# A decoder layer on one core: decay differences per head on VectorE and ScalarE, and no `wlo` of the convolution's weights on GpSimd

## The chip, the core and the metric

The kernel runs on one core of a Trainium2 chip. Five engines work side by side, each with a queue of its own that runs strictly in order: TensorE (PE; its weight loads are listed as PEld), VectorE (DVE), ScalarE (ACT), GpSimd (POOL) and SyncE (SP), which issues most of the transfers. The metric is the device time of one execution in microseconds, as a median of runs.

## The reference

One hybrid decoder layer in float32 on 256 tokens of width 1024: a half-step feed-forward part, then two token mixers side by side, cross-attention to a memory, and a second feed-forward part, each with a residual and a layer norm. The change touches one mixer, the state-space branch. Its inputs go through a causal convolution of width 4 and a silu, and its decay is a difference of running sums for each of 16 heads:

```python
def segsum(a):
    l = a.shape[-1]
    cs = jnp.cumsum(a, axis=-1)
    diff = cs[..., :, None] - cs[..., None, :]
    mask = jnp.tril(jnp.ones((l, l), dtype=bool))
    return jnp.where(mask, diff, -jnp.inf)
...
    xbc = jax.nn.silu(causal_dwconv(xbc, conv_w, conv_b))
...
    dt = jax.nn.softplus(dt_raw.astype(jnp.float32) + dt_bias)
...
    decay_in = jnp.exp(segsum(a))
    y_diag = jnp.einsum('bcgls,bgrcls,bcsgrp->bclgrp', cb, decay_in, xdt)
    decay_to_end = jnp.exp(a_cs[..., -1:] - a_cs)
```

Chunks are 128 tokens long, so there are two of them (`tb` 0 and 1 in the kernel).

## The kernel before

Every weight piece, 128x1024 in float32, is loaded into `raw` (4 buffers) by SP, rounded by ACT into `whi` and completed by `wlo = raw - whi` (6 buffers each), as `split` does at lines 150 and 151; PE multiplies in three passes (`mm3`: whi by high, whi by low, wlo by high). The subtraction runs on DVE, but `weight(ap, pool=True)` gives the second piece of a pair to POOL.

In the stage of the change, `fly` runs four streams against each other, and a scheduler then fixes the order of each engine's queue: `ssd_decay` (softplus of the time steps, their running sums `cs` by a matmul with a triangle, and the two tiles `E`), `latent` (`wb`, transposed and stored as `cTh` and `cTl`), `xbc` (the convolution), and `k_index`. `xbc` takes eight units of two pieces each, `u` = 4, 5, 6, 7 and then 0, 1, 2, 3, with POOL for the second piece of every odd `u`. The pieces are called m0 to m15 below, in the order of use, so POOL makes m3, m7, m11 and m15. Behind each unit's matmuls come, for each of two blocks of 128 channels, a bias step on ACT (line 454), three convolution steps on DVE (line 456) and a silu on ACT (line 458). Blocks 8 to 15, which come first, stay in `bcT`; blocks 0 to 7 (`wa`, 4 buffers; "token blocks" below) are transposed on PE by `flush` and copied into `xtok`.

In `ssd_decay`, POOL writes the transposed sums to DRAM (line 560), reads them back to all 128 partitions as `E` (16 heads x 128, line 562), and subtracts `cs` there (line 563). In `ssd`, DVE clips E at 0 from above (line 599), ACT takes its exponential (lines 575 and 604), and PE multiplies with it. `issue_after(x)` puts instructions of x's engine behind x in that engine's queue. The next stages take `w_qidx` and `w_ukv` pieces the same way.

Of the kernel before, what the change touches and what calls it, by code (L numbers as in the profile page):

```python
# [21 lines left out]
AF = mybir.ActivationFunctionType  # L22
ALU = mybir.AluOpType
AX = mybir.AxisListType

P = 128
# [6 lines left out]
H = 16  # L33
# [17 lines left out]
class Layer:  # L51
# [381 lines left out]
    def xbc(self, xT, xtok, bc):  # L433

        nc, t = self.nc, self.t
        late = []

        def flush(n):
            for b, v in (late.pop(0) for _ in range(min(n, len(late)))):
                tp = self.psum("t")[:, :T].rearrange("p (b c) -> p b c", c=P)  # L440
                for tb in range(NTB):
                    self.transpose(tp[:, tb, :], v[:, tb * P:(tb + 1) * P])
                nc.scalar.copy(xtok[:, :, b * P:(b + 1) * P], tp)
        for u in (4, 5, 6, 7, 0, 1, 2, 3):
            ps = self.psum("mm")
            for _ in self.a_steps(ps, t["w_xbc"][u], xT, u % 2 == 1):
                flush(max(0, len(late) - 2))
                yield 0.0
            for i in range(2):
                b = 2 * u + i  # L450
                src = ps[:, i * T:(i + 1) * T]
                v = self.small([P, T], "wa", bufs=4) if b < 8 else bc[:, b - 8, :]
                cw = self.conv_w[:, b, :]
                nc.scalar.activation(v, src, AF.Identity, bias=self.conv_b[:, b:b + 1], scale=cw[:, 3:4])
                for d in (1, 2, 3):
                    self.last_conv = nc.vector.scalar_tensor_tensor(  # L456
                        v[:, d:], src[:, :T - d], cw[:, 3 - d:4 - d], v[:, d:], op0=ALU.mult, op1=ALU.add)
                self.last_silu = nc.scalar.activation(v, v, AF.Silu)
                if b < 8:
                    late.append((b, v))  # L460
            yield 0.0
        yield "kidx"
        flush(len(late))
# [70 lines left out]
    def ssd_decay(self):  # L534

        nc = self.nc
        hb = lambda i: self.hv[:, None, i * H:(i + 1) * H].to_broadcast([P, NTB, H])
        dt = self.dtr
        nc.vector.tensor_tensor(dt, dt, hb(0), op=ALU.add)
        self.softplus(dt.rearrange("p a b -> p (a b)"), NTB * H)  # L540
        ea = self.small([P, H], "ea", bufs=1)
        nc.scalar.activation(ea, self.hv[:, H:2 * H], AF.Exp)
        dA = self.small([P, NTB, H], "dA", bufs=1)
        nc.vector.scalar_tensor_tensor(dA, dt, -1.0, ea[:, None, :].to_broadcast([P, NTB, H]),
                                       op0=ALU.mult, op1=ALU.mult)
        yield 14.0
        csp = self.psum("t")[:, :NTB * H]
        self.mm(csp, self.triu, dA.rearrange("p a b -> p (a b)"))
        cs = self.cs = self.small([P, NTB, H], "cs", bufs=1)
        nc.vector.tensor_copy(cs, csp.rearrange("p (a b) -> p a b", b=H))  # L550
        yield 1.5
        csT_p = self.psum("t")
        csT = self.small([P, T], "wa", bufs=4)[:H].rearrange("p (a b) -> p a b", b=P)
        for tb in range(NTB):
            self.transpose(csT_p[:H, tb * P:(tb + 1) * P], cs[:, tb, :])
        nc.vector.tensor_copy(csT, csT_p[:H, :T].rearrange("p (a b) -> p a b", b=P))
        scr = self.dp.tile([NTB, H * P], F32, name="cs_rows")
        self.E = []
        for tb in range(NTB):
            nc.gpsimd.dma_start(scr[tb].rearrange("(h l) -> h l", l=P), csT[:, tb, :])  # L560
            e = self.big((7, 9)[tb], F32, (P, H, P), "E")
            nc.gpsimd.dma_start(e.rearrange("p h l -> p (h l)"), scr[tb].partition_broadcast(P))
            nc.gpsimd.tensor_tensor(e, e, cs[:, tb, :].unsqueeze(2).to_broadcast([P, H, P]), op=ALU.subtract)
            self.E.append(e)

    def ssd(self, zs, xtok, bc, yT):

        nc = self.nc
        cs, E, dt, dskip = self.cs, self.E, self.dtr, self.hv[:, 2 * H:3 * H]
# [2 lines left out]
        S0, xe = sx[:, 0, :], sx[:, 1, :]  # L572
        dte, ecs = (self.small([P, H], tag, bufs=1) for tag in ("dte", "ecs"))
        with self.tc.issue_after(self.last_silu.ins):
            nc.scalar.activation(dte, E[0][:, :, P - 1], AF.Exp)
            nc.scalar.activation(ecs, cs[:, 1, :], AF.Exp)
        bcast = lambda v, n: v.unsqueeze(2).to_broadcast([P, n, HD])
        hview = lambda v: v.rearrange("p (h d) -> p h d", d=HD)
# [11 lines left out]
        for tb in range(NTB):  # L590
            ts = slice(tb * P, (tb + 1) * P)
            e = E[tb]
            cb = self.psum("t").rearrange("p (g c) -> p g c", c=P)
            for g in range(G):
                self.mm(cb[:, g, :], bc[:, g, ts], bc[:, 4 + g, ts])
            cbm = self.small([P, G, P], "w2b", bufs=2)
            nc.vector.tensor_tensor(cbm, cb, self.triu[:, None, :].to_broadcast([P, G, P]), op=ALU.mult)
            with self.tc.issue_after(self.last_conv.ins):
                nc.vector.tensor_scalar(e, e, 0.0, None, op0=ALU.min)
            yield 0.0  # L600
            for half in range(2):
                hs = slice(half * 8, half * 8 + 8)
                with self.tc.issue_after(self.last_silu.ins):
                    nc.scalar.activation(e[:, hs, :], e[:, hs, :], AF.Exp)
                ev = e[:, hs, :].rearrange("p (g r) l -> p g r l", g=2)
                nc.vector.tensor_tensor(ev, ev, cbm[:, 2 * half:2 * half + 2, :].unsqueeze(2).to_broadcast(
                    [P, 2, H // G, P]), op=ALU.mult)
            yield SSD_US[tb]
        for half in range(2):
            ps = self.psum("mm")  # L610
# [4 lines left out]
        for tb in range(NTB):  # L615
            ts = slice(tb * P, (tb + 1) * P)
            e, yt = E[tb], xtok[:, tb, :]
            for half in range(2):
                s = slice(half * 512, (half + 1) * 512)
                ps = self.psum("mm")  # L620
# [4 lines left out]
                if tb == 1:  # L625
                    po = self.psum("mm")
                    for g in (2 * half, 2 * half + 1):
# [3 lines left out]
                                            op=ALU.mult)  # L631
# [9 lines left out]
            for g in range(G):  # L641
                nc.scalar.activation(yt[:, g * 256:(g + 1) * 256], yt[:, g * 256:(g + 1) * 256], AF.Copy,
                                     scale=rs[:, g:g + 1])
# [434 lines left out]
```

## Time and profile before

| what | value |
|---|---|
| median of 3 runs | 815.27 us (815.12 to 815.87) |
| the profiled execution | 814.78 us, of which the span of the profile is 812.9 us |
| PE busy | 789.4 us, 97% of the span |
| DVE, ACT, POOL busy | 592.4, 448.4 and 68.2 us |

The profile is of one execution. Times in it count from the start of the span. A row of a timeline gives the start, the duration, the engine, the line of the kernel, the operation, `out<-in`, the shapes and, where several equal ones follow each other, their count; in brackets stands how long the engine was idle before it and what ended that. A PE row is pipelined, so rows overlap. [...] The stage of the change runs from about 227 to 290 us.

### The profile page before, as it was taken

What the parts mean: (1) busy time and instruction counts of PE and PEld (TensorE: products, weight loads), DVE (VectorE), ACT (ScalarE), POOL (GpSimd) and SP (SyncE); (2) the same over time, 40 slices, a digit from 0 to 9 for tenths busy, and PEclk for the clock granted to TensorE, in tenths of its full rate; (3) what the DMA queues carried; (4) which work ended last, traced back from release to release, by engine and by line L of the source; (5) the groups of instructions that cost most, each with busy time, mean ns of one, the idle gap of its engine ahead of it and who ended that gap; (6) DMA issues with size and microseconds to landing.
All of it is one profiled execution on the core that took longest, in us unless ns stands there. A gap on an engine that the chain in (4) does not pass through costs nothing.

```text
span 812.9 us, 13145 instructions
## 1 busy us (share of the span) xinstructions
PE 789.4 (97%) x5070; PEld 717.5 (88%) x5070; DVE 592.4 (73%) x960; ACT 448.4 (55%) x782; POOL 68.2 (8%) x69
## 2 busy tenths in 40 slices
PE   8999999999989998989999999999999999999996
PEld 5888888887889997989999998899988988888885
DVE  4868776448588989698889767965659777776445
ACT  5756565433476684477667644544444666565330
POOL 1100000000032451230000000200002000000000
PEclk9999999999999999799999999999999999999999
DMA  7876555553656621236444456574433755555531
GB/s 249 271 267 224 193 182 194 187 200 104 210 189 228 208 74 51 81 108 233 165 150 135 158 175 215 170 276 161 156 120 134 256 191 195 192 184 194 192 105 53
DMA packets 39919, 142.90 MB, mean 176 GB/s; under 512 B 4592, under 2 KB 4896, under 8 KB 39472
## 3 DMA queue, kind: packets, MB, share of 16 engines
q1 hardware_dynamic: 38016, 134.63, 49.4%
q0 software_dynamic: 1840, 7.43, 2.9%
q8 instruction: 40, 0.66, 0.3%
q14 instruction: 23, 0.19, 0.1%
HBM read 140.97 MB, written 1.06 MB: 175 GB/s over the span
## 4 chain that ended last, share of the span: by engine, by line
PE 74%; DVE 11%; issue 8%; ACT 4%; DMA 2%; POOL 1%; SPq 0%; DVEq 0%; ACTq 0%; POOLq 0%
PE ps_mm L116 69%; DVE wlo L151 3%; PE ps_t L116 2%; PE ps_t L120 2%; DMA raw<-in_ffn_in_dram 2%; ACT whi L150 1%; PE ps_s L116 1%; DVE acc L695 1%; DVE acc L702 1%; DVE wa L456 1%; DVE m L701 1%; DMA raw<-in_w_pssd_dram 0%; POOL rstd L289 0%; DVE kv L794 0%; DVE kv L793 0%
## 5 line engine op out<-in xcount | busy, mean ns | idle before, releaser
L151 DVE TENSOR_TENSOR wlo<-raw,whi 128x1024 fp32r<-128x1024 f32 (+2 forms) x245 | 301.0, 1231 | 129.1 <-ACT whi L150 125.1
L150 ACT CAST whi<-raw 128x1024 fp32r<-128x1024 f32 (+2 forms) x253 | 263.2, 1044 | 188.1 <-PE ps_mm L116 124.6
L116 PE MATMUL ps_mm<-x1T,whi 128*128 128x256 f32 x768 | 143.9, 288 | 0.0
L116 PE MATMUL ps_mm<-x0T,whi 128*128 128x512 f32 x352 | 123.7, 400 | 2.9 <-ACT whi L150 2.1
L116 PEld LDWEIGHTS ps_mm<-x1T,whi 128*128 128x128 f32 x768 | 122.3, 195 | 0.0
L116 PE MATMUL ps_mm<-x1T,wlo 128*128 128x256 f32 x384 | 110.2, 287 | 0.0
L116 PE MATMUL ps_mm<-x3T,whi 128*128 128x512 f32 x304 | 105.6, 392 | 0.0
L116 PE MATMUL ps_mm<-x0T,wlo 128*128 128x256 f32 x352 | 97.0, 282 | 0.3 <-DVE wlo L151 0.3
L116 PE MATMUL ps_mm<-x3T,wlo 128*128 128x256 f32 x304 | 85.1, 280 | 0.0
L116 PEld LDWEIGHTS ps_mm<-x0T,whi 128*128 128x128 f32 x352 | 65.8, 188 | 20.6 <-ACT whi L150 3.6
L116 PEld LDWEIGHTS ps_mm<-x1T,wlo 128*128 128x128 f32 x384 | 75.1, 195 | 0.0
L116 PEld LDWEIGHTS ps_mm<-x3T,whi 128*128 128x128 f32 x304 | 56.9, 187 | 12.4
L116 PEld LDWEIGHTS ps_mm<-x0T,wlo 128*128 128x128 f32 x352 | 65.7, 189 | 1.6 <-DVE wlo L151 1.4
L116 PE MATMUL ps_mm<-whi,ah 128*128 128x512 f32 x154 | 60.2, 391 | 0.0
L116 PE MATMUL ps_mm<-wlo,ah 128*128 128x512 f32 x154 | 60.1, 390 | 0.0
L116 PE MATMUL ps_mm<-whi,al 128*128 128x512 f32 x154 | 59.9, 389 | 0.0
L116 PEld LDWEIGHTS ps_mm<-x3T,wlo 128*128 128x128 f32 x304 | 57.5, 189 | 0.0
L289 POOL TENSOR_TENSOR rstd<-rstd,mhalf 128x1 f32<-128x1 f32 (+1 forms) x12 | 11.3, 941 | 537.0 <-DVE rstd L288 537.0
L177 DVE TENSOR_TENSOR wa<-wa,ps_mm 128x256 f32<-128x256 f32 x82 | 34.0, 418 | 30.2 <-ACT wa L176 30.1
L347 ACT ACTIVATE wa<-wa 128x256 f32<-128x256 f32 x41 | 17.1, 417 | 48.1 <-DVE wa L177 48.1
L116 PEld LDWEIGHTS ps_mm<-whi,al 128*128 128x128 f32 x154 | 28.9, 188 | 6.2
L116 PEld LDWEIGHTS ps_mm<-whi,ah 128*128 128x128 f32 x154 | 29.0, 188 | 5.6
(296 smaller groups left out, 1551.5 us busy)
## 6 DMA issues: line engine op xcount, KB each, us to landing
raw<-in_ffn_in_dram SPq DMA_DIRECT2D x87, 512.0 KB, 4.1
raw<-in_ffn_out_dram SPq DMA_DIRECT2D x44, 512.0 KB, 3.5
raw<-in_w_xbc_dram SPq DMA_DIRECT2D x16, 512.0 KB, 4.3
raw<-in_w_gate_dram SPq DMA_DIRECT2D x16, 512.0 KB, 3.4
raw<-in_w_z_dram SPq DMA_DIRECT2D x8, 512.0 KB, 3.6
raw<-in_w_qidx_dram SPq DMA_DIRECT2D x8, 512.0 KB, 3.9
raw<-in_w_q_dram SPq DMA_DIRECT2D x8, 512.0 KB, 3.5
raw<-in_w_pssd_dram SPq DMA_DIRECT2D x8, 512.0 KB, 4.6
```

Source lines behind the costliest of these rows:

```text
L116: self.nc.tensor.matmul(out, a, b, start=start, stop=stop)
L120: self.nc.tensor.transpose(out, in_, self.ident)
L150: self.nc.scalar.copy(hi, src)
L151: (engine or self.nc.vector).tensor_sub(lo, src, hi.bitcast(F32))
L177: self.nc.vector.tensor_add(out, out, ps[:, :T])
L289: self.nc.gpsimd.tensor_tensor(v, v, self.mhalf[:, :n], op=ALU.pow)
L347: nc.scalar.activation(sg, self.join(gate, sg), AF.Silu)
L456: self.last_conv = nc.vector.scalar_tensor_tensor(v[:, d:], src[:, :T - d], cw[:, 3 - d:4 - d], v[:, d:], op0=ALU.mult, op1=ALU.add)
L695: nc.vector.scalar_tensor_tensor(acc[:, s], rl[:, s], self.widx[:, tb, h:h + 1], prev[:, s], op0=ALU.mult, op1=ALU.add)
L701: nc.vector.max(m8, acc[:, s])
L702: nc.vector.match_replace(out=acc[:, s], in_to_replace=m8, in_values=acc[:, s], imm_value=KILL)
```

## The change

The subtraction of `cs` from E leaves POOL. A new method does it in the stage of the convolution: heads 0 to 7 on DVE, subtraction and clip in one instruction per head; heads 8 to 15 on ACT, as a Relu of `cs - E`, so that these hold the negative of the clipped difference, and the exponentials take a scale of -1 for them. The DVE instructions are put behind the last convolution step of units 2 and 3; the ACT instructions have no such bond. The two clips on whole tiles go. And `xbc` no longer asks for POOL, so DVE makes m3, m7, m11 and m15 too. POOL's later `wlo` pieces, of the gate weights, stay.

```diff
@@ xbc
-            for _ in self.a_steps(ps, t["w_xbc"][u], xT, u % 2 == 1):
+            for _ in self.a_steps(ps, t["w_xbc"][u], xT):
...
+            if u in (2, 3):
+                with self.tc.issue_after(self.last_conv.ins):
+                    self.decay_steps(u - 2)
             yield 0.0
@@ ssd_decay
             nc.gpsimd.dma_start(e.rearrange("p h l -> p (h l)"), scr[tb].partition_broadcast(P))
-            nc.gpsimd.tensor_tensor(e, e, cs[:, tb, :].unsqueeze(2).to_broadcast([P, H, P]), op=ALU.subtract)
             self.E.append(e)
+
+    def decay_steps(self, tb):
+
+        e, cs = self.E[tb], self.cs
+        for h in range(H // 2):
+            self.nc.vector.tensor_scalar(e[:, h, :], e[:, h, :], cs[:, tb, h:h + 1], 0.0, op0=ALU.subtract, op1=ALU.min)
+        for h in range(H // 2, H):
+            self.nc.scalar.activation(e[:, h, :], e[:, h, :], AF.Relu, scale=-1.0, bias=cs[:, tb, h:h + 1])
@@ ssd
-            nc.scalar.activation(dte, E[0][:, :, P - 1], AF.Exp)
+            for half in range(2):
+                hs = slice(half * 8, half * 8 + 8)
+                nc.scalar.activation(dte[:, hs], E[0][:, hs, P - 1], AF.Exp, scale=(1.0, -1.0)[half])
...
-            with self.tc.issue_after(self.last_conv.ins):
-                nc.vector.tensor_scalar(e, e, 0.0, None, op0=ALU.min)
...
-                    nc.scalar.activation(e[:, hs, :], e[:, hs, :], AF.Exp)
+                    nc.scalar.activation(e[:, hs, :], e[:, hs, :], AF.Exp, scale=(1.0, -1.0)[half])
```

DVE's queue where the convolution begins, before. `wlo_2374` is m6; `sps`, `spq` and `spp` are steps of the softplus behind its exponential, and `bcT` rows are convolution steps.

```order
L523 TENSOR_SCALAR sps_2100<-spe_2099 128x32
L524 RECIPROCAL sps_2100<-sps_2100 128x32
L525 TENSOR_TENSOR sps_2100<-sps_2100,spe_2099 128x32
L526 TENSOR_TENSOR spq_2101<-sps_2100 128x32
L527 TENSOR_SCALAR spp_2102<-spq_2101 128x32
L151 TENSOR_TENSOR wlo_2374<-raw_2372,whi_2373 128x1024
L529 SCALAR_TENSOR_TENSOR spp_2102<-spp_2102,spq_2101 128x32 x3
L456 SCALAR_TENSOR_TENSOR bcT_2097<-ps_mm_2140,feat,bcT_2097 128x255
L529 SCALAR_TENSOR_TENSOR spp_2102<-spp_2102,spq_2101 128x32
L456 SCALAR_TENSOR_TENSOR bcT_2097<-ps_mm_2140,feat,bcT_2097 128x254
```

The same place after the change, from the piece m6 on; `wlo_2380` is m7, formerly POOL's.

```order
L151 TENSOR_TENSOR wlo_2374<-raw_2372,whi_2373 128x1024
L526 TENSOR_SCALAR sps_2100<-spe_2099 128x32
L527 RECIPROCAL sps_2100<-sps_2100 128x32
L528 TENSOR_TENSOR sps_2100<-sps_2100,spe_2099 128x32
L529 TENSOR_TENSOR spq_2101<-sps_2100 128x32
L530 TENSOR_SCALAR spp_2102<-spq_2101 128x32
L151 TENSOR_TENSOR wlo_2380<-raw_2378,whi_2379 128x1024
L532 SCALAR_TENSOR_TENSOR spp_2102<-spp_2102,spq_2101 128x32
L456 SCALAR_TENSOR_TENSOR bcT_2097<-ps_mm_2140,feat,bcT_2097 128x255
```

The five softplus steps now stand behind m6, not ahead of it, m7 stands between them and the chain's multiplications, and the first convolution step follows one `spp`, not three.

ACT's queue at its first table load of this stage, before (`whi_2373` is m6; `spe` is the softplus's exponential):

```order
L490 ACTIVATE wa_2132,css_2133<-wb_2085 128x256
L522 ACT_TABLE_LOAD
L522 ACTIVATE spe_2099<-spe_2099 128x32
L150 CAST whi_2373<-raw_2372 128x1024
L150 CAST whi_2379<-raw_2378 128x1024
```

and after:

```order
L493 ACTIVATE wa_2132,css_2133<-wb_2085 128x256
L150 CAST whi_2373<-raw_2372 128x1024
L525 ACT_TABLE_LOAD
L525 ACTIVATE spe_2099<-spe_2099 128x32
L150 CAST whi_2379<-raw_2378 128x1024
```

The conversion of m6 moved ahead of the table load.

ACT's queue where the token blocks begin, after the change. `E_2415` and `E_2418` are the two E tiles, `wa_2515` and `wa_2521` the first two token blocks, `whi_2705` is m15:

```order
L454 ACTIVATE bcT_2097<-ps_mm_2371,feat 128x256
L574 ACTIVATE E_2415<-E_2415,cs_2352 128x128
L454 ACTIVATE wa_2515<-ps_mm_2454,feat 128x256
L574 ACTIVATE E_2415<-E_2415,cs_2352 128x128 x6
L458 ACTIVATE bcT_2097<-bcT_2097 128x256
L574 ACTIVATE E_2415<-E_2415,cs_2352 128x128
L150 CAST whi_2705<-raw_2704 128x1024
L458 ACTIVATE wa_2515<-wa_2515 128x256
L454 ACTIVATE wa_2521<-ps_mm_2454,feat 128x256
L574 ACTIVATE E_2418<-E_2418,cs_2352 128x128 x4
L454 ACTIVATE wa_2588<-ps_mm_2527,feat 128x256
L574 ACTIVATE E_2418<-E_2418,cs_2352 128x128 x2
```

None of the `L574` rows stood there before; the bias steps, silus and m15 between them did. Two more `L574` rows and the silu of the second token block follow.

## Rows read from the trace of the kernel before

**Rows 1.** The page, its first part: busy time, share of the span, instructions.

```profile
PE 789.4 (97%) x5070; PEld 717.5 (88%) x5070; DVE 592.4 (73%) x960; ACT 448.4 (55%) x782; POOL 68.2 (8%) x69
```

**Rows 2.** PE's timeline where it transposes in the stage of the change.

```profile
243.91 0.48 PE L120 MATMUL ps_t<-ident,wb 128*128 128x128 f32 x1 [3.10 <-DVE cTl L501]
...
270.02 0.60 PE L120 MATMUL ps_t<-ident,wa 128*128 128x128 f32 x4
...
277.39 0.44 PE L120 MATMUL ps_t<-ident,wa 128*128 128x128 f32 x2 [0.80 <-ACT wa L458]
```

**Rows 3.** Windows: length, busy us (count) by PE, PEld, DVE, ACT, POOL; clock share; DMA.

```profile
243.86:247.27 3.41, 3.35 (x16) 3.36 (x17) 3.13 (x6) 2.26 (x6) 0.00 (x0) 0.50 0.24 96
247.27:250.69 3.42, 3.42 (x31) 3.42 (x31) 2.19 (x6) 1.60 (x4) 0.22 (x1) 1.00 0.77 211
...
325.78:336.02 10.24, 10.24 (x46) 9.88 (x46) 6.67 (x12) 2.99 (x5) 0.00 (x0) 0.50 0.41 148
```

**Rows 4.** DVE's timeline.

```profile
227.41 2.14 DVE L539 TENSOR_TENSOR dtr<-dtr,hv 128x32 f32<-128x32 f32 x1
229.48 1.21 DVE L151 TENSOR_TENSOR wlo<-raw,whi 128x1024 fp32r<-128x1024 f32 x1
...
235.84 2.72 DVE L529 SCALAR_TENSOR_TENSOR spp<-spp,spq 128x32 f32<-128x32 f32 x3
...
243.52 0.34 DVE L501 SCALAR_TENSOR_TENSOR cTl<-ps_t,feat,cTh 128x128 fp32r<-128x128 f32 x1
...
265.42 2.08 DVE L151 TENSOR_TENSOR wlo<-raw,whi 128x1024 fp32r<-128x1024 f32 x1 [0.90 <-ACT whi L150]
...
268.84 2.01 DVE L151 TENSOR_TENSOR wlo<-raw,whi 128x1024 fp32r<-128x1024 f32 x1
...
272.19 3.21 DVE L151 TENSOR_TENSOR wlo<-raw,whi 128x1024 fp32r<-128x1024 f32 x1
...
291.57 1.23 DVE L599 TENSOR_SCALAR E<-E 128x2048 f32<-128x2048 f32 x1
...
296.75 3.73 DVE L695 SCALAR_TENSOR_TENSOR acc<-wa,widx,caus 128x256 f32<-128x256 f32 x2
```

**Rows 5.** POOL's timeline.

```profile
226.68 2.83 POOL L151 TENSOR_TENSOR wlo<-raw,whi 128x1024 fp32r<-128x1024 f32 x1 [0.96 <-ACT whi L150]
...
235.88 2.41 POOL L151 TENSOR_TENSOR wlo<-raw,whi 128x1024 fp32r<-128x1024 f32 x1 [2.99 <-ACT whi L150]
...
253.64 1.04 POOL L560 DMA_DIRECT2D cs_rows<-wa  x2 [0.77 <-DVE wa L556]
257.28 1.08 POOL L562 DMA_DIRECT2D E<-cs_rows  x2 [2.60 <-DMA cs_rows<-wa]
262.81 3.61 POOL L563 TENSOR_TENSOR E<-E,cs 128x2048 f32<-128x2048 f32 x1 [4.44 <-DMA E<-cs_rows]
...
269.73 4.59 POOL L563 TENSOR_TENSOR E<-E,cs 128x2048 f32<-128x2048 f32 x1
```

**Rows 6.** ACT's timeline at the exponential, the second table load, and a later pair.

```profile
232.04 0.23 ACT L522 ACTIVATE spe<-spe 128x32 f32<-128x32 f32 x1 [1.34 <-DVE spe L521]
...
240.07 1.28 ACT L458 ACT_TABLE_LOAD   x1 [2.87 <-DVE bcT L456]
...
361.94 0.63 ACT L230 ACTIVATE yTh<-ps_t,feat 128x128 fp32r<-128x128 f32 x2
```

**Rows 7.** Groups by form: count, busy us, mean ns of one, idle before.

```profile
L726 DVE TENSOR_SCALAR wa<-wa,asum 128x128 f32<-128x128 f32 x16 | 4.5, 280 | 0.0
...
L230 ACT ACTIVATE yTh<-ps_t,feat 128x128 fp32r<-128x128 f32 x16 | 5.4, 366 | 1.5 <-DVE yTl L231 1.3
...
L604 ACT ACTIVATE E<-E 128x1024 f32<-128x1024 f32 x4 | 4.1, 1053 | 0.0
```

**Rows 8.** The two transfers of line 562, from issue to landing.

```profile
DMA to landing us min/median/max: 5.5/6.9/8.4
```

**Rows 9.** One more window, with the columns of rows 3.

```profile
300.00:320.00 20.00, 17.43 (x132) 17.14 (x130) 19.64 (x27) 11.04 (x18) 4.66 (x3) 0.91 0.09 28
```

## The prediction

> **What bounds the kernel now.** I read the page first: TensorE (PE) is busy for 789.4 of 812.9 us [rows 1]. So the time can only change where PE stands still or runs at half its clock. PE's timeline, with the idle time ahead of each row, shows where that is in the stretch of the edit: 3.10 us before 243.91, behind a VectorE (DVE) result `cTl`, and 0.80 us before 277.39, behind a ScalarE (ACT) silu [rows 2]. [...] The third reading is what DVE does ahead of those waits. Some of its rows are far too long: an addition on 128x32 takes 2.14 us at 227.41, three tiny `spp` steps 2.72 us at 235.84, and `wlo`, 1.21 us at 229.48, takes 2.08, 2.01 and 3.21 us from 265.42 on [rows 4]. GpSimd (POOL) explains them: its `wlo` runs from 226.68 to 229.51 and from 235.88 to 238.29, its two E subtractions begin at 262.81 and 269.73 and last 3.61 and 4.59 us [rows 5]. The addition ends 0.04 us after POOL's `wlo`; the DVE `wlo` begun at 272.19 ends 1.08 us after POOL's E, nearly a full `wlo` later. DVE work on two SBUF inputs stands still while POOL computes. Against durations of 0.18 for a small step (the middle of the three is the long one) and 1.21 for a `wlo`, about 2.0, 2.1, 0.9, 0.8 and 2.0 us are lost, 7.8 together.
>
> **The early part: the four moved `wlo`.** The sixteen pieces of the convolution's weights are m0 to m15 in the order of use; POOL made m3, m7, m11 and m15. In the new order DVE makes m3 just ahead of the softplus chain and m7 inside it, and ACT converts m6 ahead of its table load instead of behind. Step by step, with the old durations:
> - DVE: m3 ends at 228.4, and the addition behind it no longer waits; the exponential's input is ready near 231.1.
> - ACT: `whi` of m6 waits for its transfer as before, until about 230.8, so the table load (1.28 us) now comes behind it and the exponential starts at 233.05, not 232.04 [rows 6]. This costs 1.0 us and eats the first gain.
> - DVE: m6, five softplus steps, m7 until 235.7, then `spp` and convolution steps in turn without POOL's block. The third convolution step of the first block ends at 237.5. It ended at 240.0, and ACT's second table load waited 2.87 us for it [rows 6].
> - The table load, silu, bias step and `cTh` follow by 239.9, `cTl` (0.34 us) by 240.9; it ended at 243.86 [rows 4]. PE is ready for it at 243.91 - 3.10 = 240.8.
>
> So PE's idle time there falls by 3.0 us. With it the half clock at 243.86 should not come: 16 matmuls in 3.41 us take some 1.8 to 1.9 at the full rate, which saves 1.5 us. **First term: -4.5 us.** A transpose of the `cs` sums now stands behind a `wb` transpose in PE's order, and that one waits for another `cTl`. By the same walk this `cTl` ends at 248.75 and PE comes at 248.1. **Second term: +0.7.**
>
> **The E subtractions.** They leave POOL and become 8 DVE and 8 ACT instructions on 128x128 for each of two tiles; the two `min` of 1.23 us on DVE go [rows 4]. No row has these forms. For DVE the nearest is L726, 128x128 by a column, 280 ns [rows 7]; DVE's rows overlap by about 0.07 (the one of 227.41 ends at 229.55, the next starts at 229.48), so 0.20 each and 3.2 us for 16. Bounds: 1.2 for all 16, if a slice costs its sixteenth of a `min`, and 4.5 with no overlap. For ACT the nearest is L230, 128x128 with a column as scale, 366 ns [rows 7]; two in a row take 0.63 [rows 6], so 0.27 each and 4.3 for 16. Bounds: 2.1, if a slice costs its eighth of L604's 1053 ns on 128x1024 [rows 7], and 5.9. [...]
>
> The first of ACT's sixteen waits for E to land. ACT's order is fixed, so all behind it waits too: the bias step of the first token block, m15's `whi`, and the silu that PE transposes next. POOL issued the first small transfer at 253.64, as soon as the sums were copied, E's two at 257.28, and the quicker E landed 5.5 us after its issue, the other 8.4 [rows 5, 8]. The sums come some 3.8 us earlier (4.5 - 0.7), so the first E lands near 259.0, the second near 262.4. ACT reaches its first E instruction at about 257.6 and stands 1.4 us. From the landing to the second token block's silu I count eight E instructions, two bias steps, m15's `whi`, three convolution steps on DVE, six more E instructions and the silu: 2.2 + 0.9 + 1.0 + 1.4 + 1.6 + 0.3 = 7.4, so 266.4. PE transposed both blocks at 270.02 [rows 2] and, 3.8 earlier, asks at 266.2. **Third term: +0.2.**
>
> **What DVE then gives back.** Behind this point DVE's queue holds more than before: m15, eight subtractions and, in the new order, `wlo` pieces of the next weights ahead of the last convolution steps. The 0.80 us wait at 277.39 goes with POOL's block of 272.19: -1.0 with the launch. But the walk has the silu of token block 4 at 277.4, where PE is ready at 276.3, and that of block 5 0.3 us later than PE, counted against where it stood: +1.4. **Fourth term: +0.4.** For the whole stage DVE's work changes by -7.8 + 4 x 1.21 + 3.2 - 2 x 1.23 = -2.2 us, and it starts earlier.
>
> **From 288 to the end.** DVE is the fuller engine here, 19.64 of 20 us in 300 to 320 [rows 9]. Old DVE ended its second `min` at 292.8 [rows 4]; the walk has the new one through its subtractions at 289.2 with the same weights done, 3.6 earlier. POOL keeps its multiplications and later `wlo`s; they stop `acc` again, as at 296.75, where two steps took 3.73 us [rows 4]. I take that loss as unchanged, shifted with the rest; ACT's exponentials are 4 as before. The terms sum to -4.5 + 0.7 + 0.2 + 0.4 = -3.2; DVE's side says -3.6. I take -3.4; later PE is the bound again and passes the shift on. The profiled execution took 814.78 us, which would be 811.4; the median stands 0.49 above it, so I say **811.9 us** for the median of 815.27.
>
> **Rivals.**
> - *The gain stays whole.* PE never waits for silus behind 262, because the small instructions cost their lower bounds (DVE 2.0 less, ACT 2.2 less): only the first term and the -1.0 stay, -5.5, 809.8 us. For it: POOL's blocks go where DVE was latest. One half-clock stretch fewer, like that at 325.78 [rows 3], would add up to 5.
> - *DVE eats it.* DVE must make four more `wlo` and 16 small steps before the last convolution ends; at 0.28 each the -2.2 becomes -0.9, and if the stage from 262 on ends where DVE ends, with its idle time as before, that is all: 814.4 us. For it: DVE is the fuller engine behind it [rows 9]. Against it: the blocked 7.8 us go, and DVE's start is earlier.
> - *ACT stands behind E, slower than before.* If E lands no earlier than it did (262.8), ACT stands 5.2 us, the second silu comes at 270.2, later than PE's old 270.02, and the whole 4.5 is gone; the silus of blocks 3 to 7 follow a DVE queue with two extra `wlo` (2.4 us) in front, so +2.4, 817.7 us. It decides from a landing at about 262.5 on. Against it: the transfers hang on the sums, which come earlier. [...]
>
> **How the numbers follow.** The forecast, from 809.8 to 813.6: 0.47. Whole gain or more: 0.20. DVE eats it, within 0.2% (1.6 us, about what a measurement of this kernel can tell from no change): 0.18. Slower: 0.15. Faster holds the first two and a little of the third, where the time falls under 813.6: 0.69; same 0.17, slower 0.14. The range reaches to half of the outer cases: a half-clock stretch less below, 807.0, and most of the slow case above, 816.9.
>
> **What will show it.** Right: no PE idle of 3 us before the second `wb` transpose, no half clock near 244, no DVE row of 2 us or more from 226 to 285, ACT standing 1 to 3 us before its first E instruction, and silus of blocks 4 and 5 on which PE waits up to 1 us. Wrong: E landing past 262; the idle time before `cTl` still there, which would mean that ACT's late table load and not POOL's block sets it; or half-clock stretches that come and go behind 310, which no step here foresees.

## The result, and the profile after

The changed kernel takes 806.73 us (median of 4 runs, 804.96 to 810.31), the kernel before 815.19 on the same chip (4 runs, 813.51 to 815.87): ratio 0.9892, 95% interval 0.9855 to 0.9929. The forecast had the sign and the first mechanism, but 3.4 us where 8.5 were gained; 806.7 lies just under its range. The profiled execution took 804.96 us, with a span of 803.3. It is the fastest of the four, so the shifts read from its trace sum to more than the 8.5 of the medians.

The page's first part (answers to [rows 1]):

```profile
PE 782.3 (97%) x5070; PEld 711.9 (89%) x5070; DVE 589.4 (73%) x978; ACT 452.2 (56%) x799; POOL 48.5 (6%) x63
```

PE's timeline, its waits from 236 to 360 (answers to [rows 2]):

```profile
239.87 0.33 PE L120 MATMUL ps_t<-ident,wb 128*128 128x128 f32 x1 [0.71 <-DVE cTl L504]
...
275.88 0.44 PE L120 MATMUL ps_t<-ident,wa 128*128 128x128 f32 x2 [0.64 <-ACT wa L458]
...
308.41 0.58 PE L116 MATMUL ps_s<-kidxh,w2a 128*128 128x256 f32 x1 [5.01 <-ACT wa L702]
...
354.18 0.66 PE L120 MATMUL ps_t<-ident,xtok 128*128 128x128 f32 x4 [1.72 <-DVE yTl L231]
```

The 3.10 us ahead of the `wb` transpose have become 0.71, and in 260 to 300 one wait of 0.64 is left. But behind 300 there is a wait of 5.01 us, longer than any before. The clock by windows, with the columns of [rows 3] (the clock share is of the full clock; the last two are the busy share of the DMA engines and GB/s):

```profile
239.00:249.00 10.00, 9.29 (x79) 9.10 (x78) 9.26 (x20) 7.51 (x14) 0.02 (x1) 1.00 0.56 177
...
307.10:313.93 6.83, 5.52 (x26) 5.52 (x27) 6.74 (x8) 3.39 (x8) 3.34 (x1) 0.50 0.24 77
```

No half clock near 244: the share is 1.00 from 239 to 249, where before 16 matmuls stood in 3.41 us at 0.50 and 31 in the next 3.42 us at 1.00 [rows 3]. Between 300 and 345 the kernel before had half clock for 10.24 us at 325.78 [rows 3] and for 3.41 at 312.13:

```profile
312.13:315.54 3.41, 3.41 (x19) 3.41 (x18) 3.35 (x6) 0.81 (x2) 0.00 (x0) 0.50 0.47 154
```

In this trace it is 6.83 us, once. DVE, where the convolution begins and in the E steps (answers to [rows 4]):

```profile
227.68 0.19 DVE L542 TENSOR_TENSOR dtr<-dtr,hv 128x32 f32<-128x32 f32 x1
...
237.85 0.63 DVE L532 SCALAR_TENSOR_TENSOR spp<-spp,spq 128x32 f32<-128x32 f32 x3
...
239.47 0.34 DVE L504 SCALAR_TENSOR_TENSOR cTl<-ps_t,feat,cTh 128x128 fp32r<-128x128 f32 x1
...
278.34 1.65 DVE L572 TENSOR_SCALAR E<-E,cs 128x128 f32<-128x128 f32 x8
...
285.22 1.65 DVE L572 TENSOR_SCALAR E<-E,cs 128x128 f32<-128x128 f32 x8
...
290.73 3.96 DVE L705 SCALAR_TENSOR_TENSOR acc<-wa,widx,caus 128x256 f32<-128x256 f32 x2
```

The addition of 2.14 us takes 0.19, three `spp` take 0.63 and not 2.72, and the first `cTl` ends 4.05 us earlier (239.81 for 243.86). Where POOL still multiplies (288.72 to 292.49 in its row below, with its next instruction from 292.46 to 294.54), two `acc` steps still take 3.96. ACT and POOL (answers to [rows 5] and [rows 6]):

```profile
231.22 1.28 ACT L525 ACT_TABLE_LOAD   x1
232.51 0.23 ACT L525 ACTIVATE spe<-spe 128x32 f32<-128x32 f32 x1
...
236.78 1.28 ACT L458 ACT_TABLE_LOAD   x1 [0.84 <-DVE bcT L456]
...
257.97 0.40 ACT L574 ACTIVATE E<-E,cs 128x128 f32<-128x128 f32 x1 [1.32 <-DMA E<-cs_rows]
...
258.72 1.85 ACT L574 ACTIVATE E<-E,cs 128x128 f32<-128x128 f32 x6
```

```profile
252.12 1.08 POOL L565 DMA_DIRECT2D E<-cs_rows  x2 [2.09 <-ACT whi L150]
288.72 3.77 POOL L592 TENSOR_TENSOR xdt<-xtok,dtr 128x1024 f32<-128x1024 f32 x2 [35.52 <-ACT xtok L443]
```

**Where the time went.** The 48 weight pieces on `x1T` that begin with m0 give PE's clock marks: the table has by how much PE begins a piece's first `wlo` product earlier (-) or later than in the trace of before (pieces 0, 4, 12, 14, 18 and 47 begin there at 227.24, 238.86, 267.38, 273.57, 288.19 and 466.63).

| piece | 0, 4 | 12 | 14 | 18 | 47 |
|---|---|---|---|---|---|
| changed, shift in us | -0.82 | -4.67 | -4.67 | -5.43 | -9.63 |

So 0.82 was there ahead of any edit, 3.85 came by piece 12, 0.76 from there to piece 18, and 4.20 behind it, where the forecast had nothing.

### The profile page after: what moved, and what is told of

Its sections match the earlier page's. It is cut to its first block, busy times and chain, and to the rows that moved or that the text cites. A ratio compares the mean times of both kernels' runs of the same rounds, so it can differ in the third digit from the quotient of the medians.

```text
span 803.3 us, 13174 instructions
## 1 busy us (share of the span) xinstructions
PE 782.3 (97%) x5070; PEld 711.9 (89%) x5070; DVE 589.4 (73%) x978; ACT 452.2 (56%) x799; POOL 48.5 (6%) x63
## 4 chain that ended last, share of the span: by engine, by line
PE 54%; DVE 5%; ACT 2%; issue 0%; POOL 0%; DVEq 0%; ACTq 0%
PE ps_mm L116 49%; PE ps_t L116 2%; PE ps_s L116 2%; PE ps_t L120 1%; DVE wlo L151 1%; ACT whi L150 1%; DVE acc L712 1%; DVE m L711 1%; DVE amax L731 0%; DVE oTl L151 0%; DVE yTl L231 0%; ACT kv L802 0%; ACT wa L732 0%; DVE wa L728 0%; DVE acc L705 0%
```

## The experiments

Each group of runs was made beside the kernel before, on a chip of its own. Before's median there was 816.0 to 816.6 us, and its executions spread over 809.6 to 821.0; a difference between two groups is one between medians from two chips. Three theories were to be told apart: that lifted blocks of DVE carry the whole gain; that the decay part carries the later half; and that what comes behind piece 18 has a cause of its own. The table has all runs: "profiled" is the time of the profiled execution, E the time from issue to landing of the first E transfer in it, and the columns behind are its shifts at the pieces, as above. They are of one execution: in runs 6, 14 and 16 it was 4.1, 1.6 and 3.2 us slower than the median, and its shifts overstate the loss.

| run | median | profiled | ratio to before, interval | E | 4 | 12 | 14 | 18 | 47 |
|---|---|---|---|---|---|---|---|---|---|
| changed | 806.73 | 804.96 | 0.9892 (0.9855 to 0.9929) | 5.8 | -0.8 | -4.7 | -4.7 | -5.4 | -9.6 |
| 1 | 812.40 | 813.80 | 0.9941 (0.9918 to 0.9964) | 5.6 | 0.6 | -2.7 | 1.8 | 0.3 | -0.8 |
| 2 | 820.61 | 818.18 | 1.0053 (1.0028 to 1.0079) | 8.0 | 0.0 | 0.2 | 1.4 | 2.3 | 3.5 |
| 3 | 812.84 | 812.37 | 0.9957 (0.9940 to 0.9975) | 9.4 | -1.8 | -1.7 | 0.8 | 0.6 | -2.4 |
| 4 | 817.35 | 816.28 | 1.0012 (0.9990 to 1.0034) | 9.0 | -1.7 | -5.0 | -3.1 | -2.0 | 1.6 |
| 5 | 807.26 | 808.95 | 0.9886 (0.9856 to 0.9915) | 5.8 | 0.8 | -2.6 | -2.6 | -3.4 | -5.9 |
| 6 | 815.37 | 819.42 | 0.9997 (0.9974 to 1.0021) | 8.4 | 1.6 | -2.0 | 2.3 | 0.6 | 4.8 |
| 7 | 820.69 | 821.16 | 1.0052 (1.0031 to 1.0072) | 8.0 | 1.4 | 1.6 | 3.3 | 3.8 | 6.5 |
| 8 | 809.63 | 809.63 | 0.9919 (0.9892 to 0.9946) | 5.6 | 0.4 | -3.2 | -3.1 | -3.8 | -5.0 |
| 9 | 816.39 | 816.31 | 0.9998 (0.9974 to 1.0022) | 13.8, twice read | 0.4 | -3.3 | 7.6 | 5.8 | 1.7 |
| 10 | 811.22 | 811.22 | 0.9930 (0.9897 to 0.9963) | 9.1 | 0.6 | -2.8 | 2.4 | 0.6 | -3.4 |
| 11 | 806.05 | 806.51 | 0.9874 (0.9843 to 0.9904) | 6.2 | -0.1 | -3.7 | -3.4 | -4.1 | -8.2 |
| 12 | 807.22 | 807.61 | 0.9898 (0.9864 to 0.9932) | 6.9 | 0.0 | -3.8 | -2.3 | -2.9 | -7.0 |
| 13 | 814.39 | 814.70 | 0.9978 (0.9960 to 0.9996) | 7.6 | 0.5 | 1.8 | 3.1 | 3.6 | -0.5 |
| 14 | 812.64 | 814.20 | 0.9953 (0.9933 to 0.9974) | 5.6 | -0.1 | -3.4 | -3.4 | -4.0 | -0.5 |
| 15 | 810.43 | 809.33 | 0.9935 (0.9912 to 0.9957) | 5.3 | -0.8 | -4.4 | -4.4 | -1.2 | -5.4 |
| 16 | 810.66 | 813.84 | 0.9929 (0.9905 to 0.9953) | 9.4 | 0.5 | -0.1 | 2.6 | 1.9 | -0.9 |
| 17 | 809.13 | 810.15 | 0.9913 (0.9882 to 0.9943) | 5.0 | -1.7 | -5.1 | 0.8 | -0.5 | -4.6 |
| 18 | 810.38 | 810.92 | 0.9932 (0.9911 to 0.9952) | 5.5 | 2.2 | -1.3 | -1.3 | -2.1 | -3.7 |

### Runs 1 to 4: one part, or part of one

Run 1 is the kernel before with the convolution's weights taken from POOL; run 2 the changed kernel with them given back; in runs 3 and 4 POOL makes two of the four.

```diff
 run 1, on before
-            for _ in self.a_steps(ps, t["w_xbc"][u], xT, u % 2 == 1):
+            for _ in self.a_steps(ps, t["w_xbc"][u], xT):
 runs 2, 3, 4, on the changed kernel
-            for _ in self.a_steps(ps, t["w_xbc"][u], xT):
+            for _ in self.a_steps(ps, t["w_xbc"][u], xT, u % 2 == 1):
+            for _ in self.a_steps(ps, t["w_xbc"][u], xT, u in (5, 7)):
+            for _ in self.a_steps(ps, t["w_xbc"][u], xT, u in (1, 3)):
```

> The kernel before with only the convolution's weights taken from GpSimd; the E subtraction stays on GpSimd and the two clips stay on VectorE. Theory, that GpSimd's blocks of VectorE set the waits: the 3 us of idle time before the `cTl` at 243.9 and the half clock behind it go, the gain there is 4 us, but the two E subtractions still block VectorE near 260 to 272, with four more `wlo` in its queue, so that at least the 0.8 us wait for token block 4 stays and grows: 3 to 4 us faster than before. Rival A, that the decay part carries what the prediction missed: the same 3 to 4 us, and the half clock of 10 us at 325 stays. Rival B, that the later 4 us come by themselves wherever the early part ends earlier: 8 us faster.

> The changed kernel with GpSimd making m3, m7, m11 and m15 again. Theory: the first idle time at 243.9 and its half clock stay, and the later gain comes only as far as VectorE is no longer blocked at 262 to 274: 1 to 4 us faster than before. Rival A, that the decay part carries the later gain: 4 to 5 us faster, with no half clock at 325. Rival B: about as before, as the early part is as before.

> The changed kernel with GpSimd making m3 and m7 alone again. Theory: the idle time before `cTl` comes back with 3 us and its half clock with 1.5, so 4 us slower than the changed kernel, 811. Rival, that ACT's late table load and not GpSimd's block sets the wait, or that VectorE, relieved of two `wlo`, wins elsewhere: within 1 us of the changed kernel.

> The changed kernel with GpSimd making m11 and m15 alone again. Theory: the first term stays (no idle time before `cTl`), m11 falls where VectorE has time, and m15 blocks VectorE by up to 2 us where the token blocks are convolved: 0 to 1.5 us slower than the changed kernel. Rival, that VectorE is the bound in 262 to 290 by its amount of work: 1 to 2 us faster, since two `wlo` of 1.2 us leave it.

The first term came as the theory had it: from piece 4 to 12 run 1 gains 3.3 and run 4 3.3, while runs 2 and 3, with m3 and m7 on POOL, gain nothing (0.2 later in both). But the parts do not add up: 4.0 us faster and 4.2 slower than before make 8.5 faster together, and run 4, meant to cost 0 to 1.5, cost 10. No theory had that. Two things stood out in its trace: E landed late, and PE's, DVE's and ACT's queues behind the convolution were in another order, since the scheduler sorts all that follows an edit anew.

### Runs 5 to 8: once more, and PE's later order

Run 5 is the changed kernel again. Runs 6 and 7 swap PE's order behind the convolution between the two kernels, by ordering edges that carry no wait:

```diff
+    def tie(self):
+
+        for row in ORDER:
+            for a, b in zip(row, row[1:]):
+                self.tc.add_manual_dep(self.pes[b], self.pes[a].name, mybir.DependencyInfo(
+                    mybir.DependencyClass.NoSync, mybir.DependencyReason.DATA), reason="order")
```

Run 8 takes the gate's weights from POOL too:

```diff
-            yield from self.a_steps(ps, t["w_gate"][4 * i + u], xT, i == 0)
+            yield from self.a_steps(ps, t["w_gate"][4 * i + u], xT)
```

> The changed kernel itself once more, beside the kernel before and the next three on the same chip, so that they have a common yardstick. Its gain of 8.5 us rests on four runs so far. Theory, that the gain is the kernel's and not the luck of a few executions: 7 to 10 us faster than before. Rival: 3 to 5, as forecast.

> The changed kernel with PE's queue behind the convolution tied to the order that the kernel before has there (seven places at which the two orders differ). Theory, that the 4 us gained behind 300 come from the other order of PE's queue: 3 to 5 us slower than the changed kernel, and the half clock of 10 us comes back. Rival A, that the earlier start of the stage gives them: within 1 us of the changed kernel. Rival B, that the half clock stretches fall by chance: anything, with a spread between executions as wide as the difference.

> The kernel before with PE's queue behind the convolution tied to the order that the changed kernel has there, and nothing else changed. Theory of the order: 3 to 4 us faster than before, and one half clock stretch fewer. Rival A, the earlier start: within 1 us of before, or slower, since the order fits DVE's other timing.

> The changed kernel with VectorE making the first gate's `wlo` too, which GpSimd has at 307, 323 and 341. Theory, that GpSimd's blocks set the waits wherever VectorE is full: VectorE gets 4.8 us more work and loses 5 to 6 us of standing still in 300 to 350, so 0 to 2 us faster than the changed kernel. Rival, that VectorE is the bound by its amount of work there: 1 to 4 us slower.

Run 5 repeats the gain: 9.3 us. Its trace is of its slowest execution of six: it wins 2.6 us behind piece 18, where the first trace of the changed kernel wins 4.2, and its half clock between 300 and 345 is 6.83 us in two pieces, not one. Run 6 keeps 1.2 us of the gain, which is not clear of noise, and run 7 is 4 us slower than before: PE's order alone is worth nothing, and one that the other queues do not fit costs 2.7 to 4.2 behind piece 18 in the two traces. Run 6 also differs ahead of the tie: 2.3 us later than before at piece 14, where run 5 is 2.6 earlier. ACT's timeline and PE's in run 6 show why (tied kernels have other line numbers):

```profile
263.47 0.40 ACT L587 ACTIVATE E<-E,cs 128x128 f32<-128x128 f32 x1 [4.17 <-DMA E<-cs_rows]
```

```profile
270.96 0.44 PE L133 MATMUL ps_t<-ident,wa 128*128 128x128 f32 x2 [2.52 <-ACT wa L471]
```

E landed 8.4 us after its issue and not 5.8; ACT stood 4.17 us, and PE then waited for the second token block. Run 8 is slower than run 5 by about 2 us, its rival's case: it is level until piece 18, and behind it wins only 1.2.

### Runs 9 to 12: one thing at a time

In these runs all instructions of PE, DVE and ACT were tied to the changed kernel's order, so that in these three queues nothing but the edit moves. Run 9 reads E twice, run 10 has m11 and m15 on POOL, runs 11 and 12 put back before's order at one stretch of PE's queue each.

```diff
 run 10, with all other order tied
-            for _ in self.a_steps(ps, t["w_xbc"][u], xT):
+            for _ in self.a_steps(ps, t["w_xbc"][u], xT, u in (1, 3)):
 run 9
-            nc.gpsimd.dma_start(e.rearrange("p h l -> p (h l)"), scr[tb].partition_broadcast(P))
+            for _ in range(2):
+                nc.gpsimd.dma_start(e.rearrange("p h l -> p (h l)"), scr[tb].partition_broadcast(P))
 run 11, PE's queue: seven products go behind two heads' scores
-MATMUL ps_mm<-x1T,whi 128x256 x2
-MATMUL ps_mm<-x1T,wlo 128x256
-MATMUL ps_mm<-x1T,whi 128x256 x2
-MATMUL ps_mm<-x1T,wlo 128x256
-MATMUL ps_mm<-x1T,whi 128x256 x2
+MATMUL ps_mm<-x1T,whi 128x256
 MATMUL ps_s<-kidxh,w2a 128x256
 run 12, the first of its two places
-MATMUL ps_mm<-xdt,E 128x64 x8
 MATMUL ps_s<-kidxh,w2a 128x256
 MATMUL ps_s<-kidxl,w2a 128x256
 MATMUL ps_s<-kidxh,w2a 128x256
+MATMUL ps_mm<-xdt,E 128x64 x8
```

> The changed kernel with each of the two E tiles read twice over, and the queues of PE, DVE and ACT tied to the changed kernel's order, so that nothing moves but the landing of E. In the changed kernel E landed 5.8 us after its issue and ACT stood 1.3 us; in four kernels that turned out slower it landed 8.0 to 9.4 us after its issue, ACT stood 4 to 6 and PE then waited 1.9 to 2.7 for the second token block. Theory, that the landing of E decides most of the gain: landing 3 to 4 us later, PE waits 2 to 3 us at the second token block, and all in all 4 to 8 us slower than the changed kernel, since a late stage also loses what was gained behind 300. Rival, that the late landing is only a sign and the order behind 300 decides: 2 to 3 us slower, no more.

> The changed kernel with GpSimd making m11 and m15, and every other instruction of PE, DVE and ACT tied to the changed kernel's order. The run before with the same edit and a free order was 10 us slower than the changed kernel. Theory, that the order which the scheduler gave to that run, or a late E there, cost it that: 0 to 2 us slower than the changed kernel. Rival, that GpSimd's blocks of VectorE at m11 and m15 cost it: 6 to 10 us slower.

> The changed kernel with everything tied to its own order, but for one place of PE's queue near 303 to 308: the four `w2a` and `w2e` score products of the index heads stand ahead of the piece's first products, as in the kernel before, and not behind seven of them. Theory, that this order hides seven products in a wait that comes anyway: 0.5 to 1.5 us slower than the changed kernel. Rival, that it decides the half clock at 325: 4 to 5 us slower.

> The changed kernel with everything tied to its own order, but for two places of PE's queue near 325 to 335: the products of the second E tile and of `S0xe` stand among the score products as in the kernel before. Theory, that PE's order there is worth little when DVE is ahead: within 1 us of the changed kernel. Rival, that it brings the half clock of 10 us back: 3 to 5 us slower.

Run 9 moved E's landing by 8 us, not by 3 to 4, and ACT stood 9.69 us. PE's timeline:

```profile
272.21 0.69 PE L136 MATMUL ps_t<-ident,wa 128*128 128x128 f32 x2 [5.33 <-ACT wa L474]
275.18 0.69 PE L136 MATMUL ps_t<-ident,wa 128*128 128x128 f32 x2 [2.27 <-ACT wa L474]
...
319.67 0.58 PE L132 MATMUL ps_s<-kidxh,w2a 128*128 128x256 f32 x1 [5.01 <-ACT wa L719]
```

10.9 us are lost between pieces 12 and 14 (7.6 in the two waits; the rest falls in 10.24 us of half clock from 270.82 on), and the kernel is 9 us slower than run 5. The last row is the telling one: it is the same wait of 5.01 us as at 308.41, and behind piece 18 the run wins the same 4.2 us, though it arrives there 11 us later than the changed kernel. So the expected loss behind 300 did not come, and an earlier start is not what gives those 4 us.

Run 10 costs 4 us, not 10: the other 6 of run 4 were its order. In its profiled execution the edit costs nothing up to piece 12, then 5.1, with E landing after 9.1 us. Runs 11 and 12 are level with the changed kernel, so the tying itself costs nothing here. Neither stretch of PE's queue carries the 4 us by itself, nor brings the half clock of 10 us back (by 10 us windows it sums to 6.8 us in each, between 300 and 320).

### Runs 13 to 16: the whole later order, E out of the way, the first term

Runs 13 and 14 swap the order of all three queues behind the convolution. Run 15 puts ACT's E instructions behind the silus of the third and fifth token blocks; run 16 is run 3 (`u in (5, 7)`) with everything else tied.

```diff
 run 14, ACT's queue where the convolution ends; run 13 has this the other way round
 ACTIVATE wa<-wa 128x256
 ACT_TABLE_LOAD
-ACTIVATE dte<-E 128x8
+ACTIVATE dte<-E 128x8 x2
 COPY xtok<-ps_t 128x2x128
+ACTIVATE ecs<-cs 128x16
+ACTIVATE E<-E 128x1024
 ACTIVATE w2e<-ps_mm 64x512
+ACTIVATE E<-E 128x1024 x2
 ACTIVATE w2a<-ps_mm 64x512
 ACTIVATE wa<-ps_s 128x384
-ACTIVATE dte<-E 128x8
-ACTIVATE ecs<-cs 128x16
 ...
 run 15, ACT's queue: the 16 instructions on E leave their places ...
-ACTIVATE E<-E,cs 128x128
-ACTIVATE E<-E,cs 128x128 x6
-ACTIVATE E<-E,cs 128x128
-ACTIVATE E<-E,cs 128x128 x4
-ACTIVATE E<-E,cs 128x128 x2
-ACTIVATE E<-E,cs 128x128 x2
 ... and stand behind the silus of the third and the fifth token block
+ACTIVATE E<-E,cs 128x128 x8
+ACTIVATE E<-E,cs 128x128 x8
```

The changed order thus puts ACT's steps for the index heads (`w2a`, `w2e`, `wa`) ahead of the first exponential of E; before's has three exponentials ahead of most of them.

> The kernel before, with the queues of PE, DVE and ACT behind the convolution tied to the order of the changed kernel (and its own order ahead of it); no other edit. Theory, that the order behind the convolution is worth 4 us by itself: 3 to 5 us faster than before, with PE's time lost in one idle stretch of 5 us and one half clock, and not in two and two. Rival, that it needs the changed kernel's earlier and lighter DVE: within 1.5 us of before, or slower.

> The changed kernel with the queues of PE, DVE and ACT behind the convolution tied to the order of the kernel before. Theory of the order: 3 to 5 us slower than the changed kernel, near 811 to 812, with the half clock at 325 back; what is left, 4 us below the kernel before, is the gain ahead of 300. Rival: within 1 us of the changed kernel.

> The changed kernel with ACT's eight instructions on the first E tile behind the silu of the third token block and those on the second behind that of the fifth; all other order tied. ACT no longer waits for E. Theory, that a late landing of E costs the changed kernel only in some executions: the median 0 to 1.5 us faster than the changed kernel, with no execution above 809. Rival, that the instructions only move the delay to later silus: 0.5 to 2 us slower.

> The changed kernel with GpSimd making m3 and m7, and every other instruction of PE, DVE and ACT tied to the changed kernel's order. Theory of the first term: PE's idle time ahead of the `cTl` grows by 2.5 to 3 us and the half clock comes back, 3.5 to 4.5 us slower than the changed kernel. Rival, that the place of m3 and m7 in DVE's queue and not GpSimd's block sets it: within 1 us.

Run 14 is the measurement that splits the gain: without the new later order the changed kernel is 812.64, 3.3 us below before, and 5.4 above the changed kernel of run 5. PE's waits behind 285 there, and the window of half clock:

```profile
287.32 0.44 PE L136 MATMUL ps_t<-ident,wa 128*128 128x128 f32 x2 [1.75 <-ACT wa L474]
...
307.15 0.39 PE L132 MATMUL ps_s<-kidxh,w2a 128*128 128x256 f32 x1 [1.29 <-ACT wa L718]
...
321.93 7.09 PE L132 MATMUL ps_mm<-xdt,E 128*128 128x64 f32 x32 [2.56 <-ACT S0xe L639]
```

```profile
320.43:337.50 17.07, 15.57 (x65) 14.85 (x66) 11.18 (x21) 5.45 (x11) 0.00 (x0) 0.50 0.36 117
```

Three waits of 1.3 to 2.6 us stand where the changed order has one of 5.01, and the clock is halved for 17.07 us and not 6.83. But this is the slowest of the run's nine executions, with the lowest mean granted clock, 0.987; the others had 0.989 to 0.994. Over all executions the mean granted clock was 0.989 in the kernel before (111 executions), 0.994 in the changed kernel (10) and 0.991 in run 14 (9). As a share of 812 us, and by estimate, half clock is thus worth some 4 us between before and the changed kernel, about half of the gain, and some 2.4 of the 5.4 in run 14; the rest of the 5.4 is not traced to single waits. Run 13 is the mirror: in its trace the changed order wins 4.1 us behind piece 18 in the kernel before as well, with 3.41 us of half clock there:

```profile
318.83:322.25 3.42, 3.42 (x19) 3.42 (x18) 3.36 (x4) 0.95 (x3) 0.97 (x1) 0.50 0.13 50
```

By its median it is only 1.6 us faster than before, though, less than expected: its profiled execution was 3.1 later than before's from piece 4 to 18, where no edit stands. So the rival keeps a part: by medians the order is worth 1.6 us here, 3 in run 17 below and 5.4 in run 14, though behind piece 18 it wins 4.1 in the traces of runs 13 and 17 alike. Whether the 3.1 in front is chance, the ties or the late E (7.6 us) is open.

Run 15 takes ACT's wait for E away and is 3 us slower than the changed kernel. The cost moves: eight E instructions at 276.14 last 2.44 us and PE waits at the next silu.

```profile
281.73 0.44 PE L136 MATMUL ps_t<-ident,wa 128*128 128x128 f32 x2 [2.25 <-ACT wa L474]
```

Its executions spread over only 809.3 to 812.0. In the changed kernel these instructions lie between 257.97 and 265.99, and PE was busy for all of the 15.00 us from 255 to 270. Run 16 brings POOL's blocks back (its `wlo` from 227.15 and 235.43), and with them PE's wait of 2.48 us at 242.93 and a half clock of 3.42 at 244.02: from piece 4 to 12 it gains 0.6, not 3.3 to 3.9. Its 810.66 is 3.4 above the changed kernel; a late E lies in that too.

### Runs 17 and 18: half the change with the new order, and PE's new wait

Run 17 is run 1 with the queues behind the convolution in the changed kernel's order. Run 18 moves three rows in ACT's queue.

```diff
 run 18, ACT's queue
+ACTIVATE w2a<-ps_mm 64x512
+ACTIVATE wa<-ps_s 128x384
+ACTIVATE wa<-ps_s 128x384
 CAST whi<-raw 128x1024
 ...
-ACTIVATE w2a<-ps_mm 64x512
-ACTIVATE wa<-ps_s 128x384
-ACTIVATE wa<-ps_s 128x384
```

> The kernel before with the convolution's weights taken from GpSimd and nothing else edited (E subtraction on GpSimd, clips on VectorE), with the queues of PE, DVE and ACT behind the convolution tied to the changed kernel's order. The same edit with its own order was 4 us faster than before. Theory, that the order adds its 4 to 5 us wherever it stands: 7 to 9 us faster than before, about the changed kernel's time; the decay part's own work is then worth no more than 1 to 2 us. Rival, that the order needs the lighter DVE: 3 to 5 us faster than before.

> The changed kernel with all order tied, but for ACT's queue at 303: one `w2a` step and the two score steps on which PE waits at 308.4 stand ahead of four `whi` conversions, which took from 303.48 to 307.39. Theory, that ACT's queue and nothing else holds PE there: the score steps come at about 304, PE's idle time falls from 5.2 to some 1.5 us and the half clock behind it does not come, 3 to 6 us faster than the changed kernel, 801 to 804. Rival, that DVE, busy 98% of 300 to 330, is the bound: PE waits elsewhere instead, within 1.5 us of the changed kernel.

Run 17 is 6.9 us faster than before, run 1 was 4.0: the order adds 3, just short of what was expected. The decay part's own work would be worth the 2 us that are left to the changed kernel, but the intervals of run 17 and of the changed kernel overlap, so this is not shown. Its trace shows where: POOL's E subtractions run from 257.18 to 265.34, and PE loses 5.9 us between pieces 12 and 14, where the changed kernel loses none.

Run 18 removes the 5.01 us wait and is 3 us slower:

```profile
307.92 0.38 PE L132 MATMUL ps_s<-kidxh,w2a 128*128 128x256 f32 x1 [1.23 <-ACT wa L718]
...
317.04 0.36 PE L132 MATMUL ps_s<-kidxh,w2e 128*128 128x256 f32 x1 [1.61 <-DVE w2e L694]
...
322.78 0.38 PE L132 MATMUL ps_s<-kidxh,w2e 128*128 128x256 f32 x1 [1.95 <-ACT wa L718]
```

```profile
323.38:333.62 10.24, 10.24 (x47) 9.88 (x46) 7.98 (x13) 2.17 (x5) 2.48 (x1) 0.50 0.54 205
```

PE waits as long in three places, 4.79 us, and then stands at half clock for 10.24 us: 47 matmuls, where the 10.24 us at 325.78 before the change held 46 [rows 3]. Its rival was right that PE waits elsewhere instead, and missed that the run would be 3 us slower; that DVE holds this stretch is not shown, since two of the three waits end with ACT. No run beats the changed kernel; run 11 is level with it.

## Why the prediction was wrong, step by step

- **First term, -4.5: right.** 3.3 to 3.9 us by piece 12 in each of the 13 runs in which DVE makes m3 and m7, and at most 0.6 in those in which POOL does. All links were seen: the addition without a block, the table load behind m6's `whi` (the exponential at 232.51; the walk said 233.05), the third convolution step by 236.70 (237.5), the half clock gone. In the changed kernel's trace it is 0.65 smaller, since PE still waits 0.71 us ahead of the first `cTl`. That DVE stands still beside POOL holds in before's trace, from 226 to 290, for rows whose two inputs are both SBUF tiles and that begin behind POOL's (2.01 to 3.21 us); convolution steps, with `ps_mm` for one input, took 0.47 to 0.48 us beside POOL's E subtractions, as they did without. At 342.55 it was POOL that lost: DVE's `wlo` took 1.22 us there and POOL's 3.90, against 2.41 at 235.88.
- **Second term, +0.7: wrong, small.** PE does not wait at the second `wb` transpose; the term is 0.
- **Third term, +0.2: right in the changed kernel, and fragile.** ACT stood 1.32 us (1.4 foreseen) and PE did not wait. The prices held: eight DVE instructions in 1.65 us (0.21 each, against 0.20) and six ACT instructions in 1.85, which is 0.29 each with the first one's 0.39 taken off, (1.85 - 0.39) / 5. The row that I took for ACT, 0.27, was thus 0.02 too low. Where E lands after 8 us or more (runs 2 to 4, 6, 10 and 16), PE loses 1.2 to 5.1 us between pieces 12 and 14: this is the rival in which ACT stands behind E, and run 9 shows by itself that the landing does it.
- **Fourth term, +0.4: wrong sign, -0.8.** The sums left earlier than I had them: POOL issued E at 252.12, 5.2 us earlier than before (0.8 of it ahead of any edit) and not 3.8, so E landed at 257.9 (259.0) and the silu of block 4 came at 275.41 (277.4). DVE was through its subtractions at 286.87 (289.2). Which of these brings the 0.8 was not tested.
- **"From 288 to the end", 0: this step failed.** The prediction took the loss behind 288 "as unchanged, shifted with the rest", and let PE pass the shift on. But the scheduler had sorted the queues of PE, DVE and ACT anew (PE's up to about 385), and that order wins 4.2 us here (4.0 to 4.2 in the traces of runs 9 to 13, 15 and 17 too, 2.6 and 2.8 in those of runs 5 and 16). Run 9 shows that it does not come from starting earlier, run 14 that with the old later order the changed kernel gains 3.3, close to the 3.4 of the sum; the order is the other 5.4, from medians of two chips. That 3.3 comes so close is in part luck: in its trace the part in front of piece 18 wins 3.9, more than the sum, and 3.5 are lost again behind it. The prediction named "half-clock stretches that come and go behind 310, which no step here foresees" as what would make it wrong. That is what happened: in the two traces 13.65 us of half clock became 6.83, and half of the difference, 3.4 us, would be most of the 4.2; that is an estimate, from 16 and 19 matmuls in 3.41 us of half clock and 31 in 3.42 us of full clock in the kernel before.

Among the rivals, "the gain stays whole" was nearest, but its reason (smaller prices of the small instructions) was not the cause; its added half-clock stretch was in part. (The range took half of that stretch's 5 us off 809.8, which is 807.3 and not 807.0.) Open is which rows of the new order carry the gain: PE's alone do not (runs 7, 11 and 12), and before's whole order on PE under the new one on the other two queues was not tried, since the queues would wait for each other. Open is too what makes E land after 5 to 7 us in some traces and after 7.6 to 9.4 in others.

## What to carry to other kernels

Where a scheduler orders the queues, an edit reaches as far as its order differs: read the order of all busy engines up to the row from which it is the same again, and take no stretch as shifted that was sorted anew. To price one edit, tie every other instruction to the order it had; the same edit cost 10 us with a free order and 4 with a tied one. And count waits by where they fall: one of 5.01 us stood here with 6.83 us of half clock in the kernel of 806.73 us, and three that sum to 4.79 and 5.60 with 10.24 and 17.07 in those of 810.38 and 812.64 (runs 18 and 14).

## What the hardware did that was not expected

- **Half clock was shorter with one long wait of PE than with three short ones.** With 5.01 us in one wait, up to 308.41, it lasted 6.83 us; with 4.79 us in three waits (run 18) 10.24; with 5.60 in three (run 14, the first of them at 287) 17.07, each in one execution. By 10 us windows, in the traces of the two kernels and of runs 5 to 18: in eleven of the sixteen, among them the changed kernel's, PE stands still for 3.8 to 5.8 us between 300 and 320, and half clock between 300 and 350 sums to 3.4 or 6.8 us; in five (before, runs 6, 7, 14 and 18) PE stands still there for 1.2 to 2.8 us, and half clock sums to 10.2 to 17.1. Which of the two brings the other is not shown.
- **The same transfer landed after 5.0 to 9.4 us.** The two E tiles have the same size and queue in all runs, and the first landed 5.0 to 6.9 us after its issue in eleven traces, before's among them, and 7.6 to 9.4 in eight (run 9 left out). The difference goes with POOL's pieces: of the eight kernels in which POOL makes some of m3, m7, m11 and m15, seven land late, all but before; of the eleven others one does, run 6. So the late E in runs 4, 10 and 16 may belong to what they change and not to chance; no run separates the two. In run 6 the busy share of the DMA engines falls to 0.09 at 265 and 0.06 at 266, and the second tile lands at 267.56; of 16 engines these shares would be the work of 1.4 and 1.0, by estimate:

```profile
264.00:265.00 1.00, 1.00 (x10) 1.00 (x10) 0.64 (x2) 1.00 (x4) 0.00 (x0) 1.00 0.27 102
265.00:266.00 1.00, 1.00 (x11) 1.00 (x10) 0.96 (x3) 1.00 (x5) 0.00 (x0) 1.00 0.09 37
266.00:267.00 1.00, 1.00 (x11) 1.00 (x10) 0.14 (x1) 1.00 (x4) 0.00 (x0) 1.00 0.06 25
```

In the changed kernel the share falls from 0.97 to nothing within 2 us:

```profile
260.00:261.00 1.00, 1.00 (x10) 1.00 (x10) 0.60 (x2) 1.00 (x4) 0.00 (x0) 1.00 0.97 393
261.00:262.00 1.00, 1.00 (x11) 1.00 (x10) 0.00 (x0) 1.00 (x2) 0.00 (x0) 1.00 0.56 225
262.00:263.00 1.00, 1.00 (x11) 1.00 (x10) 0.85 (x1) 1.00 (x4) 0.00 (x0) 1.00 0.01 4
```

What these rows show is the end of the second tile; what delays the first is open. The late landing of run 6 came without a longer issue, and DVE was idle in the last 3 us of it: POOL's issue of the two transfers took 1.08 us in both kernels and in run 6 too, and in run 6 DVE stood idle for 3.98 us, up to 264.36, while the first tile was still on its way until 263.45.
